# RWKV-7/gMLP block, MLA and HGRN2 on one core: the B branch's gates queued beside the inverses, and the output projection's inputs loaded one step sooner

## The chip, the cores and the metric

The kernel runs on one core of one Trainium2 chip (trn2). The metric is the device time of one execution in microseconds (us); a lower time is better. Names of engines: PE is TensorE (matmuls), DVE is VectorE, ACT is ScalarE, POOL is GpSimd, SP is SyncE, which here only issues transfers (DMA).

## The reference, cut to what matters

Two blocks run one after the other on 512 tokens of width 1024, all in float32. The change lies in the first block, whose branches share one input `h`:

```
h = x * (1 + scale) + shift                  # from silu(c) @ w_ada
p = h @ w_in                                 # 1536 columns for A, 2176 for B
out_a = gelu(u) * mix(layer_norm(gelu(v))) * silu(gate)      # A branch
# B branch, RWKV-7, 8 heads of 64, after a token shift:
S = S * w_t + (S a_t) b_t^T + v_t k_t^T ;  y_t = S r_t       # per head, over 512 tokens
y = (layer_norm(y) + bonus) * silu(gate)
o = concat(out_a, y) @ w_out
x = layer_norm(ALPHA * x + gate * o)
```

The second block (latent attention, two MLPs, HGRN2) follows with the same `x` and is not touched.

## The kernel before

Each float32 product is made of three matmuls of rounded parts (`mm3`): high weight with high activation, high with low, low with high. A weight tile of 1024x128 is loaded whole (`wload`, 512 KB, issued by SP, `raw`), rounded by ACT (`wh`, a CAST), and its remainder made by DVE (`wl`). `raw` and the pair `wh`/`wl` have three buffers each. One product of 1024x128 weights with all 512 tokens is 8 *steps* of three 128x512 matmuls; its sum lies in a PSUM tile `mm` (two buffers in this stage). `wprio` sets how far ahead of time the loads are scheduled.

The recurrence is done in 8 pieces of 64 tokens (`NC_R`). First DVE inverts 32x32 triangles for all pieces at once (`inverse`, L788: 31 pairs of multiply and add on `XT`, `TV`, `us`), and the result goes through DRAM (`scT`) to the tiles `Tst` and `TTb` of each piece (`tload`, eight loads of 16 KB; two sets of buffers, so that piece c+2 waits for piece c's `merge`). `merge(c)` makes the inverse of a 64x64 block: PE on `Tst`, DVE `Psb`, PE on `TTb`, ACT copies the result (`TTn`, named `XT` in the profile). Then PE turns `V` and `BK`, which ACT copies to `TV`, `Bt`, `Kt`. `chain(c)` is the recurrence: PE `sd`, ACT copy `ds`, PE `su`, DVE `us`, PE `ss` and `sd` again, ACT copy `Yt`, ACT and DVE update `S`.

Other products fill PE's time. They wait in a Python list `queue`; `fill(n)` takes n steps out of it into the program. While DVE inverts, `fill(NFILL)` puts in the first steps; later `chain(c)` yields three times and `fill(FILLS[c][i])` puts steps between. The queue holds four `ugate` products pairs of the A branch (4 x 16 steps) and four `gate` products of the B branch (8 steps each). `gate(i)` (L676) loads `bz` (one buffer, from DRAM `bonD`), makes its product, and at its end queues one float32 matmul of `bz` with a block matrix `bo` on PE (a *bonus matmul* below; it shows as `mg<-bz,bo`, two records), then a token shift (ACT `sh`, DVE `gsh`), a tanh and three more passes (`gt`, `gsh`, `gbn`), and writes `G2D` and `B2D` to DRAM.

`out_gate` (L931) is a part of the modulation: 512 KB of `w_ada` in `raw`, summed by DVE in eight instructions (`ga`). `operands` (L958) loads the A branch's result (`oaD`) back and splits it (ACT `aH`, DVE `aL`), after which the output projection (weights `w_out`, matmuls of 128x256) can begin on its first half; the step after which this is put in is `OPC`. All PE work of this stage carries one order token (`petoken`), so that PE keeps the order in which it is written down, except for the output projection, which the scheduler puts where it expects room. Each engine's list of instructions is fixed when the program is built.

Of the kernel before, what the change touches and what calls it, by code (L numbers as in the profile page):

```python
# [36 lines left out]
EARLY = 3  # L37
UNITS = ((0, 1), (1, 1), (2, 2), (4, 2), (6, 2))
TT = ("sm", "sm", "mm", "mm")
NFILL = 69  # L40
ORDER = "r0 A0 k1 g0 k2 r1 g0 n0 r2 f11 g0 f1 t0 g1 m0 g1 k3 g1 g2 l0 g2 r3 g3 l1 g2 f5 l2 f2 g3 l3 f3 l4 f2 g3 l5 f3 l6 f3 l7"
ORDER = [(z[0], int(z[1:])) for z in ORDER.split()]
OPC = 3
OG = (2, 2, 1, 0, 1, 0, 0, 0)
FILLS = [(0, 3, 5), (0, 3, 5), (2, 5, 3), (2, 6, 5)] + [(0, 0, 0)] * 4
HALVES = (slice(0, T // 2), slice(T // 2, T))


# [13 lines left out]
class Kern:  # L62
# [238 lines left out]
    def block1(self):  # L301
# [175 lines left out]
        def shift_evac(ps, mc, out, v3=False):  # L477

            sh = shs[0]
            shs.append(shs.pop(0))  # L480
            self.act(sh[:, 1 : T + 1], ps, AF.Copy, scale=self.pc("mu_b", mc))
            o3 = lambda a: a.rearrange("p (c t) -> p c t", t=RC) if v3 else a
            self.stt(out, o3(ps), omu[:, mc : mc + 1], o3(sh[:, 0:T]), ALU.mult, ALU.add)
# [174 lines left out]
        def part_gemm(w, col0, evac, leng=None):  # L658
            wh, wl = self.wchunk(w, col0, 8, P, leng)
            ps = self.ptl("mm")  # L660
            for k in range(8):
                self.mm3(ps, wh[:, k, :], wl[:, k, :], h.hi(k), h.lo(k), k == 0, k == 7)
                if k == 7:
                    with tc.high_priority(self.wprio):
                        evac(ps)
                yield
# [9 lines left out]
        def gate(i, pool):  # L676
            bz = self.tl(pool, [P, T], "bz", bufs=1)
            nc.sync.dma_start(out=bz, in_=bonD[i])

            def evac(ps):  # L680
                psb = self.ptl("mg")
                self.mm(psb, self.bo, bz)
                bn = self.tl(pool, [P, T], "gbn", bufs=1)
                self.tt(bn, psb, V[i], ALU.mult)
                g = self.tl(pool, [P, T], "gsh", bufs=2)
                shift_evac(ps, 12 + i, g)
                t = self.tl(pool, [P, T], "gt", bufs=2)
                self.act(t, g, AF.Tanh, scale=0.5)
                self.stt(t, t, 1.0, g, ALU.add, ALU.mult)
                self.act(t, t, AF.Copy, scale=0.5)  # L690
                self.act(g, t, AF.Copy, scale=self.pc("gn_g", i))
                nc.sync.dma_start(out=G2D[i], in_=g)
                self.stt(bn, bn, self.pc("gn_b", i), t, ALU.add, ALU.mult)
                nc.sync.dma_start(out=B2D[i], in_=bn)

            yield from part_gemm(w_in, 3072 + i * P, evac)
# [22 lines left out]
        queue = []  # L719

        def fill(n):

            while n > 0 and queue:
                if next(queue[0], "end") == "end":
                    queue.pop(0)
                else:
                    n -= 1
# [47 lines left out]
        rp = rx_.enter_context(self.pool("rw", 1))  # L775
# [190 lines left out]
        self.petoken = "block1"  # L966
        queue += [ugate(j, rp) for j in range(4)]
        self.psums([("mm", 2), ("mg", 2), ("sd", 2), ("su", 1), ("ss", 1)])
        queue.append(gate(0, rp))
        self.wprio = 3000  # L970
        fill(NFILL)
        self.wprio = 400
# [15 lines left out]
        with first():  # L988
            for _ in between(0, ()):
                pass  # L990
        for i in range(1, 4):
            queue.append(gate(i, rp))
        posts, ogs = [], []

        def start(n):
# [7 lines left out]
        for c in range(NC_R):  # L1003
            late = [posts.pop(0) for _ in range(LATE[c])]
            steps = chain(c, between(c + 1, late))
            while True:
                with first():
                    i = next(steps, None)
                if i is None:
                    break  # L1010
                fill(FILLS[c][i])
            if c in POSTS:
                posts.append(post(POSTS.index(c)))
                with first():
                    next(posts[-1])
            if c == OPC:
                while queue:
# [830 lines left out]
```

## Time and profile before

| | us |
|---|---|
| median of 3 runs | 1593.04 (1591.77 to 1593.08) |
| the profiled execution | 1593.87 |
| its span in the trace | 1591.8 |
| PE busy | 1530.3 (96%) |
| DVE busy | 908.4 (57%) |
| ACT busy | 714.2 (45%) |
| granted PE clock, mean | 0.989 |

The span is the time from the first to the last instruction of the trace; the profiled execution was about 2 us longer, and 0.8 us longer than the median. Busy time of PE is that of its matmul records, whose ends are modelled, so a busy PE is not one at its peak. Times within the trace count from the span's start. The changed stage lies between about 200 and 300 us.

### The profile page before, as it was taken

The page shows a single profiled execution, that of the slowest core. Times are in us where ns is not written, and L with a number is a line of the kernel's source. Part 1 is how long each engine was busy: PE and PEld are TensorE (multiplying, and loading weights), DVE is VectorE, ACT ScalarE, POOL GpSimd, SP SyncE. Part 2 cuts the span into 40 slices and gives each one's busy share as a digit, 9 for nine tenths or more (in the row PEclk, how much of TensorE's full clock was granted, in tenths as well). Part 3 has the DMA queues.
Part 4 walks back from the last instruction along what each step waited for, and adds up shares of the span by engine and source line. Part 5 has one row for each costly group of instructions (what it writes and reads, how often), then busy time and mean ns, then how long its engine had stood idle before and what let it go on. Part 6 is the DMA issues. An engine that isn't in the chain of part 4 may idle for free.

```text
span 1591.8 us, 21985 instructions
## 1 busy us (share of the span) xinstructions
PE 1530.3 (96%) x8389; PEld 1299.7 (82%) x8389; DVE 908.4 (57%) x1613; ACT 714.2 (45%) x1302; POOL 255.6 (16%) x418
## 2 busy tenths in 40 slices
PE   5899989989999999999999999999999999999997
PEld 4787778889878899888888887888888988888886
DVE  6767677667668738333343456667755714343445
ACT  3544226545666656332232335667645624332232
POOL 3212010324300032000000033223324100000000
PEclk9999999999999999999999999999999999999999
DMA  9632556532133133333333232322213224232421
GB/s 313 193 104 85 113 156 183 156 110 70 54 78 91 39 99 87 100 96 102 93 93 103 82 104 60 110 73 79 68 54 106 93 67 120 80 105 66 132 80 53
DMA packets 260828, 161.17 MB, mean 101 GB/s; under 512 B 29553, under 2 KB 241124, under 8 KB 260724
## 3 DMA queue, kind: packets, MB, share of 16 engines
q1 hardware_dynamic: 258036, 153.40, 33.4%
q0 software_dynamic: 2544, 6.11, 1.4%
q8 instruction: 66, 1.08, 0.3%
q14 instruction: 38, 0.31, 0.1%
q10 hardware_dynamic: 144, 0.26, 0.0%
HBM read 146.90 MB, written 11.53 MB: 100 GB/s over the span
## 4 chain that ended last, share of the span: by engine, by line
PE 68%; DVE 4%; issue 2%; ACT 1%; DMA 1%; POOL 1%; SPq 0%; DVEq 0%; POOLq 0%; ACTq 0%
PE mm L143 59%; PE sm L143 5%; PE po L143 2%; PE sc L143 1%; DVE bL L133 1%; DVE res L123 1%; DVE wl L123 1%; DMA sw<-tr 0%; PE pt L1377 0%; PE sm L149 0%; DVE mlom L133 0%; DVE hgmm L133 0%; POOL tr L123 0%; PE kv L143 0%; DVE mlpy L123 0%
## 5 line engine op out<-in xcount | busy, mean ns | idle before, releaser
L140 ACT CAST wh<-raw 128x1024 fp32r<-128x1024 f32 (+3 forms) x244 | 242.4, 995 | 475.9 <-PE mm L143 380.1
L123 DVE TENSOR_TENSOR wl<-raw,wh 128x1024 fp32r<-128x1024 f32 (+3 forms) x244 | 287.6, 1180 | 292.3 <-ACT wh L140 288.7
L143 PE MATMUL mm<-bL,wh 128*128 128x512 f32 (+1 forms) x752 | 279.1, 374 | 0.8 <-DVE bL L133 0.8
L143 PE MATMUL mm<-bH,wl 128*128 128x512 f32 (+1 forms) x752 | 278.1, 372 | 0.0
L143 PE MATMUL mm<-bH,wh 128*128 128x512 f32 (+1 forms) x752 | 276.9, 375 | 0.5 <-ACT t L137 0.4
L143 PE MATMUL mm<-aH,wh 128*128 128x512 f32 (+1 forms) x656 | 240.3, 368 | 5.8 <-ACT gsh L137 3.2
L143 PE MATMUL mm<-aL,wh 128*128 128x512 f32 (+1 forms) x656 | 238.3, 364 | 0.0
L143 PE MATMUL mm<-aH,wl 128*128 128x512 f32 (+1 forms) x656 | 237.2, 363 | 0.2 <-DVE wl L123 0.2
L143 PEld LDWEIGHTS mm<-bL,wh 128*128 128x128 f32 x752 | 141.1, 188 | 25.0 <-DVE bL L133 1.3
L143 PEld LDWEIGHTS mm<-bH,wl 128*128 128x128 f32 x752 | 141.2, 188 | 24.8
L143 PEld LDWEIGHTS mm<-bH,wh 128*128 128x128 f32 x752 | 139.4, 188 | 26.0 <-ACT t L137 0.8
L143 PEld LDWEIGHTS mm<-aH,wh 128*128 128x128 f32 x656 | 125.6, 192 | 27.5 <-ACT gsh L137 3.6
L143 PEld LDWEIGHTS mm<-aH,wl 128*128 128x128 f32 x656 | 125.6, 192 | 19.8 <-DVE wl L123 0.6
L143 PEld LDWEIGHTS mm<-aL,wh 128*128 128x128 f32 x656 | 126.0, 192 | 17.7 <-issue 0.2
L143 PE MATMUL mm<-wh,aH 128*128 128x512 f32 x288 | 113.5, 396 | 1.7 <-ACT aH L140 1.7
L143 PE MATMUL mm<-wl,aH 128*128 128x512 f32 x288 | 113.3, 395 | 0.0
L143 PE MATMUL mm<-wh,aL 128*128 128x512 f32 x288 | 109.3, 395 | 0.0
L140 ACT CAST aH<-t 128x512 fp32r<-128x512 f32 (+1 forms) x74 | 41.0, 564 | 75.2 <-DVE t L123 75.1
L143 PEld LDWEIGHTS mm<-wh,aH 128*128 128x128 f32 x288 | 54.7, 190 | 14.2 <-ACT aH L140 1.8
L123 DVE TENSOR_TENSOR aL<-t,aH 128x512 fp32r<-128x512 f32 (+1 forms) x74 | 45.0, 617 | 36.9 <-ACT aH L140 36.9
L143 PEld LDWEIGHTS mm<-wh,aL 128*128 128x128 f32 x288 | 54.4, 190 | 12.4
L143 PEld LDWEIGHTS mm<-wl,aH 128*128 128x128 f32 x288 | 54.6, 190 | 12.1
(548 smaller groups left out, 2593.5 us busy)
## 6 DMA issues: line engine op xcount, KB each, us to landing
raw<-in_mlp_w_dram SPq DMA_DIRECT2D x128, 512.0 KB
raw<-in_hgrn_w_in_dram SPq DMA_DIRECT2D x32, 512.0 KB
raw<-in_w_in_dram SPq DMA_DIRECT2D x23, 512.0 KB
ada<-in_w_ada_dram SPq DMA_DIRECT2D x16, 512.0 KB
raw<-in_w_out_dram SPq DMA_DIRECT2D x10, 512.0 KB
raw<-in_w_ada_dram SPq DMA_DIRECT2D x8, 512.0 KB
raw<-in_mla_w_o_dram SPq DMA_DIRECT2D x8, 512.0 KB
raw<-in_hgrn_w_o_dram SPq DMA_DIRECT2D x8, 512.0 KB
```

Source lines behind the costliest of these rows:

```text
L123: self.st((eng or self.nc.vector).tensor_tensor(out=out, in0=a, in1=b, op=op))
L133: self.st(self.nc.vector.scalar_tensor_tensor(out=out, in0=a, scalar=s, in1=b, op0=op0, op1=op1))
L140: self.st(self.nc.scalar.copy(out=out, in_=in_))
L143: i = self.nc.tensor.matmul(out, l, r, start=start, stop=stop, **kw)
```

## The change

All four `gate` products are put in the queue before `fill(NFILL)`, which now takes 80 steps in place of 69: the 64 of the A branch and two whole gates. The other 16 steps go between the first three pieces, 6, 6 and 4 of them (before: 8, 8, 10 and the last one). `operands` is put in after piece 2 in place of piece 3.

```
-NFILL = 69
+NFILL = 80
...
-OPC = 3
+OPC = 2
 OG = (2, 2, 1, 0, 1, 0, 0, 0)
-FILLS = [(0, 3, 5), (0, 3, 5), (2, 5, 3), (2, 6, 5)] + [(0, 0, 0)] * 4
+FILLS = [(0, 3, 3), (0, 3, 3), (0, 2, 2)] + [(0, 0, 0)] * 5
...
         queue += [ugate(j, rp) for j in range(4)]
         self.psums([("mm", 2), ("mg", 2), ("sd", 2), ("su", 1), ("ss", 1)])
-        queue.append(gate(0, rp))
+        queue += [gate(i, rp) for i in range(4)]
         self.wprio = 3000
         fill(NFILL)
...
             for _ in between(0, ()):
                 pass
-        for i in range(1, 4):
-            queue.append(gate(i, rp))
         posts, ogs = [], []
```

How this moves instructions, at three places.

**Place 1, PE and SP at the end of the fill.** On PE, before, the fifth step of gate 0 (tile `mm_1978`) is followed by the merge of piece 0:

```order
L143 MATMUL mm_1978<-aL_134,wh_1974 128x512
L143 MATMUL mm_1978<-aH_126,wl_1975 128x512
L143 MATMUL mg_2007<-Tst_1548,M_330_2002 128x64 x4
L143 MATMUL mg_2014<-TTb_1550,Psb_2012 64x128 x4
L149 MATMUL mg_2020<-ident,V_101 64x128
```

After the change the last step of gate 1 (tile `mm_2026`) and its bonus matmul stand there:

```order
L143 MATMUL mm_2026<-aH_129,wl_2023 128x512
L143 MATMUL mg_2051<-bz_2018,bo 128x512
L143 MATMUL mg_2079<-Tst_1548,M_343_2074 128x64 x4
L143 MATMUL mg_2086<-TTb_1550,Psb_2084 64x128 x4
L149 MATMUL mg_2092<-ident,V_101 64x128
```

So nine matmuls (three steps) of gate 0 and 24 of gate 1, with two bonus matmuls, moved from between the pieces to ahead of the first merge, and the merge stands behind the second load of `bz`. On SP, the loads of weights around the end of the inverse (`in_w_in` are weights of gates, `in_w_ada` is `out_gate`) change places:

```order
 L161 DMA raw_1972<-in_w_in_dram 128x8x128
-L934 DMA raw_2036<-in_w_ada_dram 128x8x128
+L161 DMA raw_2020<-in_w_in_dram 128x8x128
 L714 DMA oaD<-gt_1815 128x512
-L934 DMA raw_2047<-in_w_ada_dram 128x8x128
-L161 DMA raw_2159<-in_w_in_dram 128x8x128
+L934 DMA raw_2108<-in_w_ada_dram 128x8x128
+L934 DMA raw_2119<-in_w_ada_dram 128x8x128
 L714 DMA oaD<-gt_1889 128x512
 L806 DMA scT<-TV_1542 128x1024
```

Gate 1's weights moved ahead of two loads of `w_ada`. Some 20 loads later, behind the loads of `Tst` and `TTb` of pieces 0 and 1, SP has after the change (before, piece 2's eight loads of `Tst` and `TTb` stand between the second and the third of these rows, and no load of `bz` is there):

```order
L816 DMA Tst_1549<-scT 32x4x32
L817 DMA TTb_1551<-scT 32x4x32
L714 DMA oaD<-gt_1963 128x512
L934 DMA raw_2238<-in_w_ada_dram 128x8x128
L678 DMA bz_2018<-bonD 128x512
L934 DMA raw_2249<-in_w_ada_dram 128x8x128
L161 DMA raw_2332<-in_w_in_dram 128x8x128
L692 DMA G2D<-gsh_2007 128x512
```

The load of `bz` for gate 1 is queued behind those of pieces 0 and 1, a write of `oaD` and a load of `w_ada`.

**Place 2, DVE ahead of the first `Psb`.** `Psb` is the step of the merge that PE waits for. Before:

```order
L133 SCALAR_TENSOR_TENSOR gt_1963<-mx_1896,gt_1963 128x512
L133 SCALAR_TENSOR_TENSOR ga_339_2049<-raw_2047,sc,ga_339_2049 128x128 x3
L128 TENSOR_SCALAR ga_364_2189<-raw_2187,sc 128x128
L123 TENSOR_TENSOR Psb_2012<-mg_2007,ist 128x256
L133 SCALAR_TENSOR_TENSOR ga_364_2189<-raw_2187,sc,ga_364_2189 128x128 x7
```

After:

```order
L133 SCALAR_TENSOR_TENSOR gsh_2007<-mm_1978,omu,sh_605 128x512
L123 TENSOR_TENSOR gbn_2005<-mg_2003,V_101 128x512
L133 SCALAR_TENSOR_TENSOR gt_2010<-gt_2010,gsh_2007 128x512
L128 TENSOR_SCALAR ga_373_2240<-raw_2238,sc 128x128
L133 SCALAR_TENSOR_TENSOR gbn_2005<-gbn_2005,pb,gt_2010 128x512
L133 SCALAR_TENSOR_TENSOR ga_373_2240<-raw_2238,sc,ga_373_2240 128x128 x6
L133 SCALAR_TENSOR_TENSOR gsh_2055<-mm_2026,omu,sh_606 128x512
L133 SCALAR_TENSOR_TENSOR ga_373_2240<-raw_2238,sc,ga_373_2240 128x128
L123 TENSOR_TENSOR Psb_2084<-mg_2079,ist 128x256
```

The third load of `w_ada` (`raw_2238`, the one just ahead of `bz_2018` on SP) is now read ahead of `Psb`, with all eight instructions of its sum and parts of gates 0 and 1.

**Place 3, ACT in the recurrence, from `Yt` of piece 1 to `ds` of piece 2.** Before:

```order
L140 COPY Yt_2058<-sd_2209 64x512
L140 COPY TV_1653<-mg_2299 64x4x64 x2
L140 CAST wh_2445<-raw_2443 128x1024
L137 ACTIVATE S_1_1553<-S_0_1552,PC_105 128x128
L140 COPY Bt_1544<-mg_2306 64x4x64 x2
L140 COPY Kt_1546<-mg_2306 64x4x64 x2
L137 ACTIVATE S_1_1555<-S_0_1554,PC_106 128x128
L137 ACTIVATE S_1_1557<-S_0_1556,PC_107 128x128
L137 ACTIVATE S_1_1559<-S_0_1558,PC_108 128x128
L137 ACTIVATE gt_2274<-gt_2274 128x512
L137 ACTIVATE gsh_2271<-gt_2274,pb 128x512
L140 COPY ds_2379<-sd_2368 64x512
```

After (the last rows of the same piece; `Yt`, `TV` and the cast `aH_2522` stand ahead of them):

```order
L140 COPY Kt_1546<-mg_2366 64x4x64 x2
L137 ACTIVATE S_1_1553<-S_0_1552,PC_105 128x128
L137 ACTIVATE S_1_1555<-S_0_1554,PC_106 128x128
L140 CAST aH_2524<-raw_2538 128x512
L137 ACTIVATE S_1_1557<-S_0_1556,PC_107 128x128
L137 ACTIVATE S_1_1559<-S_0_1558,PC_108 128x128
L137 ACTIVATE gsh_2319<-gt_2322,pb 128x512
L140 CAST aH_2526<-raw_2544 128x512
L140 CAST aH_2528<-raw_2544 128x512
L140 COPY ds_2424<-sd_2413 64x512
```

A weight cast left this place, and the four casts of the A branch's result came in, all ahead of `ds`.

## Rows read from the trace of the kernel before

**Rows 1.** Windows: us; busy PE, PEld, DVE, ACT, POOL; clock; DMA share; GB/s.

```profile
213.90:235.00 21.10, 16.22 (x84) 12.87 (x84) 13.53 (x35) 6.44 (x13) 4.53 (x9) 0.84 0.60 172
235.00:300.00 65.00, 64.93 (x445) 56.19 (x444) 47.23 (x112) 39.20 (x80) 13.85 (x21) 1.00 0.71 208
```

**Rows 2.** Timeline of PE: start, us, instruction, count [idle before <-releaser].

```profile
199.65 0.39 PE L143 MATMUL mm<-aH,wh 128*128 128x512 f32 x1
...
213.70 0.39 PE L143 MATMUL mm<-aH,wl 128*128 128x512 f32 x1
217.26 0.50 PE L143 MATMUL mm<-aH,wh 128*128 128x512 f32 x1 [3.17 <-ACT gsh L137]
...
223.51 1.08 PE L143 MATMUL mg<-Tst,M 128*128 128x64 f32 x8 [0.94 <-DMA Tst<-scT]
...
236.26 1.02 PE L143 MATMUL mg<-bz,bo 128*128 128x512 f32 x2
...
243.45 1.05 PE L143 MATMUL sd<-TV,res 128*128 128x128 f32 x8
```

**Rows 3.** Windows over PE's slow stretches, columns as in rows 1.

```profile
218.80:222.10 3.30, 3.30 (x9) 2.58 (x8) 3.05 (x11) 0.00 (x0) 0.00 (x0) 0.50 0.74 186
...
225.50:229.00 3.50, 3.39 (x17) 2.48 (x16) 2.18 (x6) 1.79 (x5) 1.05 (x3) 0.52 0.23 35
```

**Rows 4.** Timeline of ACT around PE's first gap.

```profile
215.66 1.04 ACT L140 CAST wh<-raw 128x1024 fp32r<-128x1024 f32 x1 [10.62 <-DMA raw<-in_w_in_dram]
```

**Rows 5.** Timeline of SP's queue, 201 to 232 us.

```profile
201.74 0.37 SPq L934 DMA_DIRECT2D raw<-in_w_ada_dram  x1
...
211.53 0.37 SPq L161 DMA_DIRECT2D raw<-in_w_in_dram  x1
...
222.48 0.43 SPq L816 DMA_DIRECT2D Tst<-scT  x1
...
225.80 0.43 SPq L817 DMA_DIRECT2D TTb<-scT  x1
...
230.25 0.38 SPq L714 DMA_DIRECT2D oaD<-gt  x1
...
231.20 0.85 SPq L161 DMA_DIRECT2D raw<-in_w_in_dram  x1
```

**Rows 6.** Window over transfers issued at 230 to 231 us, columns as in rows 1.

```profile
232.30:236.00 3.70, 3.70 (x24) 3.11 (x23) 0.91 (x2) 0.58 (x1) 1.54 (x4) 1.00 1.04 277
```

**Rows 7.** Timeline of DVE ahead of the first merge.

```profile
218.75 1.90 DVE L133 SCALAR_TENSOR_TENSOR ga<-raw,sc,ga 128x128 f32<-128x128 f32 x5
...
224.63 0.42 DVE L123 TENSOR_TENSOR Psb<-mg,ist 128x256 f32<-128x256 f32 x1
```

**Rows 8.** Timelines of DVE, ACT and PE, piece 1 to piece 2.

```profile
248.91 0.69 DVE L123 TENSOR_TENSOR us<-su,bo 128x512 f32<-128x512 f32 x1 [0.35 <-PE su L143]
...
254.95 0.59 ACT L140 COPY Yt<-sd 64x512 f32<-64x512 f32 x1 [0.63 <-PE sd L143]
...
261.45 0.58 ACT L140 COPY ds<-sd 64x512 f32<-64x512 f32 x1
...
264.68 1.16 PE L143 MATMUL su<-ds,XT 64*128 64x128 f32 x8
...
270.41 1.65 ACT L140 CAST aH<-raw 128x512 fp32r<-128x512 f32 x3
```

**Rows 9.** Timelines of DVE, SP, ACT and PE, piece 2 to the first output products.

```profile
265.88 0.69 DVE L123 TENSOR_TENSOR us<-su,bo 128x512 f32<-128x512 f32 x1
...
272.23 1.57 SPq L161 DMA_DIRECT2D raw<-in_w_out_dram  x2
...
278.05 1.03 ACT L140 CAST wh<-raw 128x1024 fp32r<-128x1024 f32 x1
...
279.11 1.22 DVE L123 TENSOR_TENSOR wl<-raw,wh 128x1024 fp32r<-128x1024 f32 x1 [0.52 <-ACT wh L140]
...
280.91 0.28 PE L143 MATMUL mm<-aH,wh 128*128 128x256 f32 x1
```

More of the change, by code (lines that the diff above doesn't have):

```diff
@@ L39 @@
 TT = ("sm", "sm", "mm", "mm")
-NFILL = 69
+NFILL = 80
 ORDER = "r0 A0 k1 g0 k2 r1 g0 n0 r2 f11 g0 f1 t0 g1 m0 g1 k3 g1 g2 l0 g2 r3 g3 l1 g2 f5 l2 f2 g3 l3 f3 l4 f2 g3 l5 f3 l6 f3 l7"
 ORDER = [(z[0], int(z[1:])) for z in ORDER.split()]
-OPC = 3
+OPC = 2
 OG = (2, 2, 1, 0, 1, 0, 0, 0)
-FILLS = [(0, 3, 5), (0, 3, 5), (2, 5, 3), (2, 6, 5)] + [(0, 0, 0)] * 4
+FILLS = [(0, 3, 3), (0, 3, 3), (0, 2, 2)] + [(0, 0, 0)] * 5
 HALVES = (slice(0, T // 2), slice(T // 2, T))
@@ L968, in block1 @@
         self.psums([("mm", 2), ("mg", 2), ("sd", 2), ("su", 1), ("ss", 1)])
-        queue.append(gate(0, rp))
+        queue += [gate(i, rp) for i in range(4)]
         self.wprio = 3000
@@ L990, in block1 @@
                 pass
-        for i in range(1, 4):
-            queue.append(gate(i, rp))
         posts, ogs = [], []
```

## Prediction

> **What bounds the kernel now.** I read the page's busy times first: PE works in 1530.3 of 1591.8 us, so time is won only where PE is idle or slow, or lost where a change makes it idle. Then the windows around the changed stage [rows 1]: from 235 to 300 us, which is most of the recurrence, PE is busy in 64.93 of 65 us at full clock, while DVE (47 us) and ACT (39 us) have room; but from 213.9 to 235 us it is busy in only 16.2 of 21.1 us. So before the change the recurrence itself has no gap to give back; all that can be won lies in the 21 us around the end of the inverse. All that the change moves is PE work, and its amount stays: the question is where PE waits.
>
> The timeline of PE shows the gaps [rows 2]: 3.17 us until 217.26, for ACT's `gsh`, and 0.94 us until 223.51, for the loads of `Tst`. The first is no lack of work. ACT had the gelu (`gsh`) to do, but ahead of it in its list stood the cast of gate 1's weights, which waited for a transfer issued at 211.53 and landed at 215.66 [rows 4, 5]; the gelu frees the PSUM buffer that gate 0's product needs. A slow clock follows: the granted clock is 0.50 (1.2 in place of 2.4 GHz) from 218.8 to 222.1 and 0.52 from 225.5 to 229 [rows 3]; before the first fall PE had stood 3.17 us, before the second it had two shorter waits.
>
> **Prices.** A 128x512 matmul costs 0.227 us when nothing waits: 62 of them lie between the starts at 199.65 and 213.70 [rows 2]. A bonus matmul of `bz` costs 1.02 us [rows 2].
>
> **Part 1, up to the first matmul of piece 1 (`sd`, 243.45 [rows 2]).** At that point PE has done 39 gate matmuls and one bonus matmul since 213.93, where the last product of the A branch ends; after the change it has done 66 and two. The same work would be done before at 243.45 + 27 x 0.227 + 1.02 = 250.6. That is the mark to compare with. Now the changed order, step by step.
>
> *The first gap goes.* Gate 1's weights are loaded in the place of the `w_ada` load of 201.74 [rows 5], ten us earlier than at 211.53. With the 4.1 us that the load of 211.53 took until ACT used it, they are there at 206, before the buffers that the cast needs are free. So ACT does its gelu in time, gate 0 starts at 213.93 and its 24 matmuls end at 219.4, the bonus matmul at 220.4, and gate 1's 24 at 225.8. (The remainder of its weights, `wl`, keeps its place on DVE right behind the inverse, which is early enough.) This is 3.2 us won, and the clock has no reason to fall here.
>
> *A new wait takes its place.* Behind gate 1 on PE stands its bonus matmul, and behind that the whole merge. `bz` has one buffer, so its second load can only be issued after the first bonus matmul, at 220.4; but it also stands in SP's list behind 16 small loads, a write and a `w_ada` load. The small loads are issued 0.47 us apart (eight from 222.48 to 225.80 [rows 5]). Piece 2's eight, which stood ahead of the write of `oaD` at 230.25, now stand behind it, and the list may run up to 0.9 us earlier, because the entry ahead of the small loads now waits for a `wl` that comes a us sooner. So the write comes 3.9 to 4.8 us earlier, at 225.8 (middle), the `w_ada` load at 226.3 and `bz` at 226.8. What such a train takes is shown at 230.25 to 231.20 [rows 5]: write, `w_ada`, weights, of which the last two (1.05 MB) moved from 232.3 to 236.0 at 277 GB/s [rows 6], so 1.85 us for 512 KB. Shifted by 4.4 us, `w_ada` is in at 229.8 and the 256 KB of `bz` at 230.7. PE thus stands from 225.8 to 230.7, ends the bonus matmul at 231.7 and the first merge matmuls at 232.8 (1.08 us [rows 2]).
>
> *DVE is later than PE.* `Psb`, on which the merge's next matmuls wait, now stands behind a whole `out_gate` sum that reads this same `w_ada` load. From 229.8: eight instructions at 0.37 (five in 1.90 [rows 7]), 2.9 us; two 128x512 passes at 0.69 (width of `us` [rows 8]), 1.4; so `Psb` at 234.1, against 233 if PE alone set it. Ahead of ACT's copy of the merge stands, in the same way, the cast of gate 3's weights, loaded one `w_ada` and one weight load behind `bz`: 230.7 + 3.7 = 234.4, cast (1.03 [rows 9]) and a tanh of about 0.6 until 236.0, some 2 us behind `Psb`, about when PE's merge delivers; I take no cost (bound: 1 us).
>
> *From `Psb` to piece 1.* Before: 243.45 - 224.63 [rows 2, 7] = 18.8 us, with 24 gate matmuls and a bonus matmul in it (6.5 us), so 12.4 without; this includes a slow clock, and I leave it in, since PE has stood longer than before (bounds: nothing, or 1.8 us more, if nine fill matmuls fall in it at twice 0.227). After: 18 gate matmuls, 4.1 us, and one pass of a gate among ACT's copies, about 0.6 (as `Yt` [rows 8]). So piece 1 starts at 234.1 + 12.4 + 4.1 + 0.6 = 251.2, which is **0.6 us later** than the mark. Bounds: 0.45 either way for SP; if DVE does not wait, 1.2 us less.
>
> **Part 2, piece 1 to piece 2.** PE reaches `su` of piece 2 earlier after `us` of piece 1, because 12 fewer gate matmuls stand between (18 in place of 30, from the two orders): before 264.68 - 248.91 = 15.8 us [rows 8], after 15.8 - 2.7 = 13.0. `su` needs ACT's `ds`. Before, ACT got there 12.5 us after `us`, six and a half after `Yt` [rows 8], with 2.6 us to spare. Its list loses a cast of weights (1.03) and gains four `aH` at 0.55 (three in 1.65 [rows 8]): 1.2 more, so `ds` starts at 13.7 and ends at 14.3. PE waits **1.3 us**. Bounds: nothing, if ACT catches up ahead of `Yt`; 2.5, if the second load of `oaD`, issued only when DVE has freed its buffer, is late too.
>
> **Part 3, piece 2 to the output projection.** Loading the operands "one step sooner" moves little: their casts already stood at 270 us [rows 8], before the end of piece 2. What the first output products wait for is their weights. Before, the load is issued 6.35 us after `us` of piece 2 (272.23 and 265.88), is cast at 12.2, and PE comes to it at 15.0 [rows 9]. SP's list between is the same kind (a `w_ada` load, piece 5's eight, a `w_ada` load), so the load stays at 6.4 after `us`; but PE, with 15 gate matmuls fewer and one merge product (1.08) behind instead of ahead, comes to it at 15.0 - 3.4 - 1.1 = 10.5. The weights land at 6.4 + 4.1 = 10.5, are cast at 11.5 and split at 12.8 (1.22 [rows 9]), and the third matmul needs the split: PE waits about **2.0 us**. Bounds: nothing, if the load goes out 2 us sooner; 3.5, if it is late by another transfer.
>
> How long a 512 KB load takes decides here. The trace has 4.1 us (211.53 to 215.66 [rows 4, 5]), and the sum goes by that. The Trainium skill, DMA: Bandwidth & Descriptors, "Anatomy of one DMA", has a fit of 2.0 us and 436 GB/s, given for POOL's path, which no run here shows for SP's loads of weights. An estimate by that page would be 3.2 us for such a load: part 3 would be 1.1 us and the whole sum 0.9 less, 3.0 us, inside what counts as no change. The measured load was slower than the page's, so the 4.1 us stand.
>
> **The sum** is 0.6 + 1.3 + 2.0 = +3.9 us. Made on the profiled execution it gives 1597.8; that execution was 0.8 us above the median of the runs shown, so on the median 1593.04 + 3.9 = **1597 us**. Behind the stage all work hangs on the recurrence's end and shifts with it.
>
> **Rivals.**
> *The fill pays.* If `bz` were there by 225.8, and DVE's sum with it, `Psb` would stand at 225.8 + 1.0 + 1.1 = 227.9, piece 1 would start at 245.0 and 5.6 us would be won: 1587.4, or 1590.7 where parts 2 and 3 still cost 3.3. For it: a gap of 3.17 us that does go. Against: SP would have to issue `bz` about 5 us sooner, and nothing in its list allows that. It decides from a landing at about 228. Chance 0.10.
> *It comes out even.* Parts 2 and 3 are hidden, because PE's order has slack I did not see, and part 1 nets out at -0.6 to 0.6: 1592 to 1594. For it: ACT and DVE are idle a quarter to 40% of the recurrence. Against: both are late by their place in the list, not by load. Chance 0.28.
> *The clock falls again and again.* Waits of 1.3 and 2 us in the recurrence bring PE to half speed as the short waits at 222 to 225 did [rows 3]. A stretch like that from 218.8 to 222.1 holds nine matmul records [rows 3], each 0.2 us dearer at half speed: 1.8 us, so two give 1600.5. Against: where PE's waits come one by one it need not fall. Chance 0.12.
>
> **How the numbers follow.** My forecast, 1595 to 1599, has 0.50. A change within 0.2% (3.2 us) is about what a measurement cannot tell from none. Slower by more than that: two thirds of the forecast and a little more (0.35), the clock rival (0.12), and upper bounds of the even case (0.03), together 0.50; the same: the rest of the forecast (0.15), of the even case (0.25) and of the fill that pays (0.03), 0.43; faster 0.07. The range leaves out the fast rival's better half and the sum of all upper bounds: 1590.5 to 1602. The forecast's own range is 1594 to 1600.
>
> **What would show it.** Right: no gap at 214 us on PE; a gap of 4 to 6 us behind gate 1, ended by `bz`; DVE's `ga` waiting for `raw<-in_w_ada` until about 230; `su` of piece 2 waiting for ACT's `ds`; the first 128x256 matmuls waiting for `wh` or `wl` of `w_out`. Wrong: `bz` landing before 228, or PE without gaps from 251 to 300 us.

## The result, and the profile after

The changed kernel takes 1599.87 us (median of five, 1598.13 to 1605.02), the kernel before took 1592.16 us beside it (five, 1588.84 to 1593.08): ratio 1.0054, 95% interval 1.0035 to 1.0072. It is slower, by more than the 0.2% that can be told from no change.

The profiled execution of the changed kernel was the fastest of its five (1598.13 us, span 1596.0), that of the kernel before (1593.87 us) was slower than all of the five beside it. The two traces thus differ by 4.2 us, not by 7.7, and 1.2 us of the 4.2 had come about before the changed stage. So all places below are counted from one landmark, DVE's copy that ends the inverse (L807). Its row before and after, from DVE's timelines:

```profile
214.59 1.03 DVE L807 COPY XT<-TV 128x1024 f32<-128x1024 f32 x1
```

```profile
215.79 1.13 DVE L807 COPY XT<-TV 128x1024 f32<-128x1024 f32 x1
```

PE's timeline after the change shows the stage (columns as in [rows 2]; "PE stands" means that it is idle ahead of an instruction):

```profile
220.52 1.02 PE L143 MATMUL mg<-bz,bo 128*128 128x512 f32 x2
...
233.04 2.07 PE L143 MATMUL mg<-bz,bo 128*128 128x512 f32 x2 [6.01 <-DMA bz<-bonD]
234.90 1.81 PE L143 MATMUL mg<-Tst,M 128*128 128x64 f32 x8
237.23 1.09 PE L143 MATMUL mg<-TTb,Psb 128*64 128x128 f32 x8 [0.52 <-DVE Psb L123]
239.32 0.63 PE L149 MATMUL mg<-ident,V 128*64 128x128 f32 x4 [1.00 <-ACT XT L140]
...
254.08 1.05 PE L143 MATMUL sd<-TV,res 128*128 128x128 f32 x8
...
273.42 1.38 PE L143 MATMUL su<-ds,XT 64*128 64x128 f32 x8 [1.04 <-ACT ds L140]
...
286.77 0.36 PE L143 MATMUL mm<-aH,wh 128*128 128x256 f32 x1
```

The gap of 3.17 us at 214 us [rows 2] is gone. In its place PE stands 6.01 us for `bz`, then works slowly (2.07 us for a bonus matmul that took 1.02, 1.81 for the merge's 1.08), and stands 1.04 us for `ds` in piece 2, which before needed no wait [rows 8]. The first output product (286.77) waits for nothing. Between the merge and piece 1, PE stands 1.00 us for ACT's copy `XT`. ACT's timeline has the freed gelu (`gsh`, right behind a cast that waits for no load; before [rows 4]), the `aH` casts ahead of `ds`, and the cast for the first output product, done before PE comes to it:

```profile
209.62 1.05 ACT L140 CAST wh<-raw 128x1024 fp32r<-128x1024 f32 x1 [3.42 <-PE mm L143]
210.57 0.59 ACT L137 ACTIVATE gsh<-mm 128x512 f32<-128x512 f32 x1
...
271.64 1.12 ACT L140 CAST aH<-raw 128x512 fp32r<-128x512 f32 x2
272.79 0.58 ACT L140 COPY ds<-sd 64x512 f32<-64x512 f32 x1
...
284.77 1.03 ACT L140 CAST wh<-raw 128x1024 fp32r<-128x1024 f32 x1
```

The weights of the output projection are there because their load goes out early: 3.5 us after DVE's `us` of piece 2, where it went out 6.4 us after it before [rows 9]. By then DVE has done the last `aL` and so has read the A branch's result out of the `raw` buffers; the load goes out right behind piece 5's small loads. DVE's timeline and SP's queue:

```profile
273.35 0.94 DVE L123 TENSOR_TENSOR aL<-raw,aH 128x512 fp32r<-128x512 f32 x1
...
275.08 0.68 DVE L123 TENSOR_TENSOR us<-su,bo 128x512 f32<-128x512 f32 x1
```

```profile
276.73 1.73 SPq L817 DMA_DIRECT2D TTb<-scT  x4
278.56 4.07 SPq L161 DMA_DIRECT2D raw<-in_w_out_dram  x2
```

Before, DVE did the `aL` only behind `us`, the first at 270.31 and three more in the row below, and the load waited on SP for one of them (1.3 us); it went out at 272.23.

```profile
271.51 1.89 DVE L123 TENSOR_TENSOR aL<-raw,aH 128x512 fp32r<-128x512 f32 x3
```

SP's queue around the merge shows why `bz` is late: it goes out behind the small loads, the write and the `w_ada` load, at 228.65 (before [rows 5]), and lands 4.4 us later.

```profile
227.70 0.38 SPq L714 DMA_DIRECT2D oaD<-gt  x1
228.12 0.43 SPq L934 DMA_DIRECT2D raw<-in_w_ada_dram  x1
228.65 0.64 SPq L678 DMA_DIRECT2D bz<-bonD  x1
```

DVE stands for that same `w_ada` load and finishes its sum 0.4 us before PE delivers to `Psb` (before [rows 7]):

```profile
232.30 0.29 DVE L128 TENSOR_SCALAR ga<-raw,sc 128x128 f32<-128x128 f32 x1 [2.88 <-DMA raw<-in_w_ada_dram]
...
236.03 0.34 DVE L133 SCALAR_TENSOR_TENSOR ga<-raw,sc,ga 128x128 f32<-128x128 f32 x1
236.75 0.42 DVE L123 TENSOR_TENSOR Psb<-mg,ist 128x256 f32<-128x256 f32 x1 [0.38 <-PE mg L143]
```

The granted clock (windows, columns as in [rows 1]) is at its lower level (0.50, 1.2 of 2.4 GHz) when PE starts again after the stand, and once more behind the wait for `ds`; elsewhere in the recurrence it is full:

```profile
233.00:236.60 3.60, 3.56 (x10) 2.45 (x10) 3.20 (x9) 0.00 (x0) 0.00 (x0) 0.50 1.15 321
236.60:254.00 17.40, 14.72 (x99) 12.33 (x99) 5.90 (x11) 9.36 (x21) 3.41 (x8) 1.00 0.48 133
...
274.20:277.60 3.40, 3.40 (x14) 2.71 (x13) 3.23 (x10) 0.58 (x1) 0.81 (x2) 0.50 0.96 246
277.60:300.00 22.40, 22.40 (x172) 20.29 (x171) 16.31 (x40) 15.48 (x33) 6.35 (x8) 1.00 0.77 229
```

### The profile page after: what moved, and what is told of

Same layout as the page of the kernel before. It is cut to its first block, busy times and chain, and to the rows that moved or that the text cites. A ratio compares the mean times of both kernels' runs of the same rounds, so it can differ in the third digit from the quotient of the medians.

```text
span 1596.0 us, 21991 instructions
## 1 busy us (share of the span) xinstructions
PE 1529.3 (96%) x8389; PEld 1299.8 (81%) x8389; DVE 908.0 (57%) x1613; ACT 713.9 (45%) x1302; POOL 256.6 (16%) x418
## 3 DMA queue, kind: packets, MB, share of 16 engines
q8 instruction: 66, 1.08, 0.3%
## 4 chain that ended last, share of the span: by engine, by line
PE 67%; DVE 5%; issue 2%; ACT 1%; DMA 1%; POOL 1%; SPq 0%; POOLq 0%; DVEq 0%; ACTq 0%
PE mm L143 58%; PE sm L143 5%; PE po L143 2%; PE sc L143 1%; DVE bL L133 1%; DVE wl L123 1%; DVE res L123 1%; DMA sw<-tr 0%; PE pt L1375 0%; PE sm L149 0%; DVE hgmm L133 0%; DVE mlom L133 0%; POOL tr L123 0%; PE kv L143 0%; SPq L1315 0%
```

## The experiments

Three theories stood against each other. *Two losses*: the fill loses at the merge (by `bz` and by DVE's sum), the operands lose at `ds`, and the clock adds to both. *One wait*: `bz` alone is the loss. *One part*: either the fill or the operands cost everything. The table has for each kernel, from its own timelines and in us:

- `Psb`: the first `Psb`, of piece 0, counted from the landmark.
- piece 1: the first `sd` of piece 1 counted from the landmark, less the kernel before (28.86) and less the gate work done earlier (27 matmuls at 0.227 and a bonus matmul, 7.15 us, as in the prediction's mark; 3.06 us for 72 steps, 6.47 for the last row). A positive number is late for equal work.
- piece 7: `su` of the last piece, where all have done the same gates, less the kernel before (118.13). (e2 has done five more output matmuls there.)
- the measured ratio to the kernel before, run beside it.

| kernel | `Psb` | piece 1 | piece 7 | ratio (95% interval) |
|---|---|---|---|---|
| before | 10.04 | 0 | 0 | 1 |
| changed | 20.96 | +2.3 | +4.8 | 1.0054 (1.0035 to 1.0072) |
| e1, `bz` early | 20.71 | +3.4 | +4.6 | 1.0032 (1.0020 to 1.0043) |
| e2, fill alone | 21.67 | +4.0 | +6.1 | 1.0037 (1.0024 to 1.0049) |
| e3, operands alone | 9.95 | -0.4 | +6.9 | 1.0037 (1.0021 to 1.0054) |
| e4, 72 steps | 13.47 | +7.7 | +10.2 | 1.0063 (1.0047 to 1.0079) |
| e5, `Psb` first | 20.42 | +1.5 | +5.5 | 1.0051 (1.0034 to 1.0067) |
| e6, one early sum | 10.34 | +0.7 | +2.2 | 1.0014 (1.0003 to 1.0024) |
| e7, 72 steps, `Psb` first | 8.48 | -3.3 | +9.1 | 1.0058 (1.0044 to 1.0073) |
| e8, own `gbn` | 15.81 | -3.1 | 0.0 | 1.0019 (1.0006 to 1.0032) |
| e9, 72 steps, casts later | 9.33 | +6.8 | +13.1 | 1.0112 (1.0097 to 1.0128) |
| e10, e8 and casts later | 13.33 | -1.9 | -0.7 | 1.0022 (1.0010 to 1.0034) |
| e11, e10, 5+5+6 steps | 13.38 | +0.6 | +1.7 | 1.0018 (1.0007 to 1.0030) |

Each kernel has one trace. The changed kernel and e2 hold the same instructions in the same order up to piece 1, and yet e2 is 1.7 us later there; its clock is at 0.50 from 230.8 to 244.5 us, that of the changed kernel from 229.8 to 236.7. So differences of less than about 2 us between rows of the table show nothing.

**e1.** The changed kernel; `bz` of gates 1 and 2 in the two buffers of tag `mx`.

```
-            bz = self.tl(pool, [P, T], "bz", bufs=1)
+            bz = self.tl(pool, [P, T], "mx", bufs=2) if i in (1, 2) else self.tl(pool, [P, T], "bz", bufs=1)
```

> The changed kernel, with the bz tiles of gates 1 and 2 in buffers of another tag, so that the load of bz need not wait for the first bonus matmul. Theory (PE's wait for bz hides a second wait, of DVE's Psb for the third sum of w_ada): the stand of 6.0 us ahead of the second bonus matmul shrinks below 1 us, but PE then stands some 5 us ahead of TTb's matmuls, because Psb stays at 235 to 236.5; piece 1 starts at most 1.2 us earlier, and the time is 1598.5 to 1600 where the changed kernel has 1599.9. Rival (bz alone is the loss): Psb at about 231, piece 1 some 5 us earlier, the time 1594 to 1596.

`Psb` did not move (20.71 against 20.96). PE and DVE now, from their timelines:

```profile
231.12 0.28 DVE L128 TENSOR_SCALAR ga<-raw,sc 128x128 f32<-128x128 f32 x1 [1.98 <-DMA raw<-in_w_ada_dram]
...
234.19 0.42 DVE L123 TENSOR_TENSOR Psb<-mg,ist 128x256 f32<-128x256 f32 x1
```

```profile
234.66 1.97 PE L143 MATMUL mg<-TTb,Psb 128*64 128x128 f32 x8 [6.60 <-DVE Psb L123]
```

The stand of 6.01 us for `bz` became one of 6.60 us for `Psb`, which waits behind the sum of a `w_ada` load. *One wait* is refuted. The ratio is lower than the changed kernel's, but the intervals overlap, and at piece 7 the traces agree within 0.2 us.

Two more readings of e1 are used below: the wait for `ds` in piece 2, and the load of the output projection's weights against PE's coming to the first output product. DVE's, SP's and PE's rows:

```profile
273.85 0.68 DVE L123 TENSOR_TENSOR us<-su,bo 128x512 f32<-128x512 f32 x1
```

```profile
276.50 3.52 SPq L161 DMA_DIRECT2D raw<-in_w_out_dram  x2
```

```profile
272.19 1.16 PE L143 MATMUL su<-ds,XT 64*128 64x128 f32 x8 [1.04 <-ACT ds L140]
...
284.15 0.36 PE L143 MATMUL mm<-aH,wh 128*128 128x256 f32 x1
```

PE comes to the first output product 10.3 us after `us`, the load goes out 2.65 us after `us`, and that product waits for nothing.

**e2 and e3.** The two parts apart: the changed kernel with `OPC = 3`, and the kernel before with `OPC = 2`.

> The changed kernel with its fill, but the operands put in after piece 3 as before. Theory (two losses of about equal size, one in the fill, one from the operands' casts ahead of ds): su of piece 2 waits less than 0.3 us for ds, no slow clock between 265 and 280 us, and the time is 1595 to 1597.5, 2.5 to 4 us below the changed kernel. Rival A (the fill alone is the loss): 1599 to 1600.5. Rival B (the operands alone are the loss): 1591.5 to 1593.

> The kernel before with its fill, but the operands put in after piece 2. Theory (the casts are late only because the change took 12 gate matmuls from ahead of su; before there were 2.6 us to spare): ds is ready within 0.5 us of PE, and the time is 1591 to 1594, the same as before. Rival (the operands cost by themselves): a wait of 1 to 2 us ahead of su of piece 2 with a slow clock behind it, 1595 to 1597.

e2 is as its theory said in the trace: `su` of piece 2 does not wait, because two of the four `aH` casts stand ahead of `ds` in place of all four, and PE is at full clock (1.00 from 272 to 278 us). ACT's and PE's rows of e2:

```profile
272.31 1.12 ACT L140 CAST aH<-raw 128x512 fp32r<-128x512 f32 x2
273.45 0.58 ACT L140 COPY ds<-sd 64x512 f32<-64x512 f32 x1
```

```profile
274.08 1.16 PE L143 MATMUL su<-ds,XT 64*128 64x128 f32 x8
```

Its ratio is 0.17% below that of the changed kernel, but the intervals overlap. So of *one part*, that the operands are everything is refuted, since the fill alone costs 0.37%; that the fill is everything is not refuted by the times. What the operands add is shown by the traces only: the wait for `ds`, in the changed kernel and e1 and not in e2.

e3 should have cost nothing and costs 0.37% too. Its `su` of piece 2 waits for nothing, but this does not test the theory: the scheduler put all four `aH` casts behind `ds` there, as in the kernel before [rows 8]. What waits are the first output products, for `wh` and `wl` of `w_out`, and a long slow stretch follows. ACT's and PE's timelines and a window of e3:

```profile
261.95 0.58 ACT L140 COPY ds<-sd 64x512 f32<-64x512 f32 x1
...
269.93 0.62 ACT L140 CAST aH<-raw 128x512 fp32r<-128x512 f32 x1 [0.87 <-DMA raw<-in_w_ada_dram]
...
281.79 1.04 ACT L140 CAST wh<-raw 128x1024 fp32r<-128x1024 f32 x1 [1.90 <-DMA raw<-in_w_out_dram]
```

```profile
282.88 0.39 PE L143 MATMUL mm<-aH,wh 128*128 128x256 f32 x1 [1.62 <-ACT wh L140]
...
284.40 0.39 PE L143 MATMUL mm<-aH,wl 128*128 128x256 f32 x1 [0.75 <-DVE wl L123]
```

```profile
285.00:295.20 10.20, 10.20 (x46) 9.30 (x45) 6.71 (x15) 3.48 (x5) 6.68 (x8) 0.50 0.74 207
```

Waits of 1.62 and 0.75 us, then 10.2 us at clock 0.50. The wait is the one of the prediction's part 3, but not for its reason. PE comes to the product 14.8 us after `us` of piece 2 (266.45), as before (15.0 [rows 9]) and not early; the load goes out 9.6 us after `us` (276.02, before 6.4), because the `w_ada` load ahead of it on SP waited 4.8 us for a sum of DVE.

**e4.** The changed kernel with 72 steps, gate 1 between the pieces.

```
-NFILL = 80
+NFILL = 72
...
-FILLS = [(0, 3, 3), (0, 3, 3), (0, 2, 2)] + [(0, 0, 0)] * 5
+FILLS = [(0, 3, 5), (0, 3, 5), (0, 4, 4)] + [(0, 0, 0)] * 5
```

> The changed kernel with 72 steps in the fill in place of 80 (gate 0 whole, gate 1 between the pieces), and the first three pieces with 8, 8 and 8 steps. Theory (PE stands for the second bz and the third sum of w_ada; without a second bonus matmul ahead of the merge it waits for neither): no stand of over 2 us between 220 and 235 us, piece 1 starts at most 0.5 us behind the kernel before measured by equal work, and with the casts still ahead of ds the time is 1592 to 1596. Rival (the first gap of 3.17 us returns, or DVE's sum still stands ahead of Psb): 1596 to 1600.

Not better than the change (1.0063, the intervals overlap), and 10.2 us late at piece 7: the theory's 1592 to 1596 is far off. No second bonus matmul stands ahead of the merge, but the gap for `gsh` is back (3.04 us), and ACT's cast of a later gate's weights, waiting for its load, stands ahead of `Bt` and `Kt`:

```profile
233.77 1.04 ACT L140 CAST wh<-raw 128x1024 fp32r<-128x1024 f32 x1 [1.21 <-DMA raw<-in_w_in_dram]
```

```profile
217.43 0.80 PE L143 MATMUL mm<-aH,wh 128*128 128x512 f32 x1 [3.04 <-ACT gsh L137]
...
236.27 1.42 PE L143 MATMUL ss<-TV,Kt 128*128 128x128 f32 x8 [3.18 <-ACT Kt L140]
```

**e5, e8, e10, e11.** The fill with `OPC = 3`, one wait after the other taken away. e5: e1's edit, and the first `Psb` ahead of all sums by an order token on DVE. e8: for gate 1 `gbn` in a buffer of its own as well (and `bz` only for gate 1). e10: casts of later weights behind ACT's copy of the first merge. e11: e10 with other steps.

```
+            self.token = "inverse" if c == 0 else None        # e5, around Psb
             self.tt(Psb, q4(ps[:, : 4 * RC]), ist.unsqueeze(1).to_broadcast([P, 4, RC]), ALU.add)
+            self.token = None
...
-                bn = self.tl(pool, [P, T], "gbn", bufs=1)     # e8
+                bn = self.tl(pool, [P, T], "mx", bufs=2) if i == 1 else self.tl(pool, [P, T], "gbn", bufs=1)
...
+            self.token = "xt" if c == 0 else None             # e10, and on later casts of weights
             self.copy(at(TTn[c % 2]), ps2[0:64, :])
+            self.token = None
...
-FILLS = [(0, 3, 3), (0, 3, 3), (0, 2, 2)] + [(0, 0, 0)] * 5
+FILLS = [(0, 2, 3), (0, 2, 3), (0, 3, 3)] + [(0, 0, 0)] * 5
```

> The changed fill with the operands after piece 3 (as in the run of the fill alone), bz of gates 1 and 2 in buffers of another tag, and the first Psb kept ahead of all sums of w_ada on DVE by an order token. Theory (the fill loses only by two waits, for bz and for DVE's sum of w_ada, and pays once both are gone): no stand of over 1.5 us on PE between 214 and 235 us, Psb at 229 to 231, full clock from 235 to 265 us, and 0 to 4 us below the kernel before of the same call, some 6 us below the fill alone. Rival A (the work comes too early for the recurrence in any case, so that its copies and loads are late): 2 us or more above the kernel before. Rival B (the sums that were pushed behind Psb make us or wl late in the recurrence): a new stand of over 1 us on PE between 235 and 300 us that DVE ends, 2 to 5 us above the kernel before.

> The run with the first Psb kept ahead of all sums, and now gate 1's gbn in a buffer of its own too (that of another tag), because there DVE stood 4.5 us for the write of gate 0's gbn, with Psb behind it. Theory (three waits stood one behind the other: bz, the sum of w_ada, and the one buffer of gbn; with the third gone the fill pays up to the recurrence): Psb at 230.5 to 232.5 us, PE's stand ahead of TTb below 3 us, piece 1's first sd at 247 to 250 us where that run has 254, and 3 to 7 us below that run (0.5% above the kernel before), so within 0.2% of the kernel before or up to 0.2% below it. Rival A (a fourth wait takes the place): Psb after 234 us, behind another load or buffer. Rival B (the early gain is given back in the pieces, because the sums and gate 3's weights come later): Psb early, but piece 4's su no more than 2 us earlier than in that run, and the time over 0.3% above the kernel before.

> The run with the gbn buffer, and on ACT the casts of later weights kept behind the copy of the first merge by an order token, because there the evacuation of gate 0 stood behind the cast of gate 2's weights (landed at 224 us), and Psb behind that on DVE. Theory (a fourth wait): Psb at 228.5 to 230.5 us, PE's stand of 3.2 us ahead of TTb below 1.5 us, piece 1 some 2 us earlier, and 1 to 3 us below the run with the gbn buffer, level with the kernel before or up to 0.15% below it. Rival (gate 2's weights or the sums are then late in pieces 0 and 1, and the pieces give back what the merge wins): a new stand of over 1 us between 232 and 265 us, and no lower than the run with the gbn buffer.

> The same with the 16 steps of gates 2 and 3 put between the pieces as 5, 5 and 6 in place of 6, 6 and 4, so that piece 2 has more of PE's work beside its waits. Theory: the small stands of piece 2 (0.85 us for Psb, 0.4 for issue) shrink, and 0 to 1.5 us below the other run of this call. Rival: the pieces are set by ACT and DVE, and the time is within 1 us of the other run.

In e5 no sum stands ahead of `Psb`, and `Psb` is still at 20.42. DVE stands for the write of gate 0's `gbn`, whose only buffer gate 1 needs (`B2D`, in SP's list behind the small loads):

```profile
236.29 0.69 DVE L123 TENSOR_TENSOR gbn<-mg,V 128x512 f32<-128x512 f32 x1 [4.54 <-DMA B2D<-gbn]
236.90 0.41 DVE L123 TENSOR_TENSOR Psb<-mg,ist 128x256 f32<-128x256 f32 x1
```

```profile
237.37 1.97 PE L143 MATMUL mg<-TTb,Psb 128*64 128x128 f32 x8 [7.87 <-DVE Psb L123]
```

A third wait, so e5's theory of two fell. With the third gone (e8) PE's stand falls from 7.87 to 3.21 us and `Psb` comes 4.6 us sooner; piece 1 is 3.1 us ahead of equal work, and the ratio falls to 1.0019. Up to piece 1 the fill does pay. At piece 7 that is lost again. From `sd` of piece 1 to `su` of piece 7 PE is idle for 4.9 us in e8, partly in small waits that the kernel before does not have (0.85 us for `Psb`, 0.51 and 0.42 of its own issue), and for 2.8 us in the kernel before; that is 2.0 of the 3.1 us. The stand ahead of `TTb` is still 3.21 us, in e8:

```profile
232.08 1.97 PE L143 MATMUL mg<-TTb,Psb 128*64 128x128 f32 x8 [3.21 <-DVE Psb L123]
```

e10 takes that away too, and PE then waits 0.80, 2.33 and 1.64 us, for `Psb`, for the copy of the merge and for `TV`, because gate 1's passes, and behind the copy a cast of weights, stand ahead of these on ACT. One of the passes stands 3.21 us for a write of `gt`, a fifth wait in the row:

```profile
234.62 0.63 ACT L137 ACTIVATE gt<-gsh 128x512 f32<-128x512 f32 x1 [3.21 <-DMA oaD<-gt]
```

```profile
237.16 0.66 PE L149 MATMUL mg<-ident,BK 128*128 128x128 f32 x4 [2.33 <-ACT XT L140]
239.45 0.97 PE L143 MATMUL sd<-TV,res 128*128 128x128 f32 x4 [1.64 <-ACT TV L140]
```

The time did not fall further (1.0022, 1.0018). In e10 the rival held: new stands of over 1 us. e11 is 0.9 us below e10, which fits its theory and its rival alike. (e10's profiled execution, 1598.77 us, is long although its trace is 0.7 us ahead at piece 7, because its landmark lies at 219.38, 4.8 us later than before.)

**e6, e7, e9.** The kernel before with one early sum of `w_ada` in place of two, which brings gate 1's weights one place forward; e7 also with 72 steps and e5's token, e9 with 72 steps and e10's token.

```
-OG = (2, 2, 1, 0, 1, 0, 0, 0)
+OG = (2, 2, 2, 0, 1, 0, 0, 0)
...
-        start(2)
+        start(1)
```

> The kernel before with one sum of w_ada started ahead of the recurrence in place of two (the other after piece 2), so that gate 1's weights are loaded one place earlier. Theory (the stand at 214 us lies beside the way of the inverse through DRAM, which sets the first merge): the stand for gsh at 214 us falls from 3.2 us below 0.5, PE stands some 4 us ahead of Tst's matmuls in its place, and the time is within 1.5 us of the kernel before. Rival (the stand at 214 us is lost time, as the prediction's part 1 took it): Tst's matmuls start 2 to 3 us earlier and the time falls by 2 to 4 us.

> The kernel before with one early sum of w_ada in place of two, 72 steps in the fill (gate 0 whole with its bonus matmul, 3.1 us more work ahead of the merge), and the first Psb ahead of all sums of w_ada by an order token. Theory (the time between the inverse and Tst's landing is 4 us of idle PE, and 3.1 us of work that waits for nothing fits in): no stand of over 1.5 us between 214 and 235 us, piece 1's start level with the kernel before although 3.1 us more is done, and 2 to 4 us below the kernel before. Rival (ACT's casts and DVE's sums, now later, are late for the pieces): a stand of over 1 us between 228 and 260 us, and the time from 1 us below to 5 us above the kernel before.

> The kernel before with one early sum of w_ada in place of two, 72 steps in the fill, and on ACT the casts of later weights kept behind the copy of the first merge by an order token (Psb without a token). Theory (5.45 us of PE's idle time ahead of Tst's matmuls take 3.1 us of work, if no cast or sum stands ahead of the merge's own steps): piece 1 starts within 0.5 us of the kernel before although 3.1 us more is done, and if gate 1's weights are not late for piece 0, 1 to 3 us below the kernel before. Rival (gate 1's weights, now cast behind the merge, make PE stand in piece 0): a stand of over 1 us for wh or wl between 228 and 236 us, a slow clock behind it, and 0 to 5 us above the kernel before.

e6 shows what the first gap was worth by itself: nothing. It is gone, and PE stands for `Tst` in its place:

```profile
224.40 1.94 PE L143 MATMUL mg<-Tst,M 128*128 128x64 f32 x8 [5.45 <-DMA Tst<-scT]
```

`Psb` comes at 10.34 from the landmark, before at 10.04: the way of the inverse through DRAM sets it. (At 1.0014 e6 is within the 0.2% of the kernel before.) e7 fills these 5.45 us with 3.1 us of work, and up to piece 1 it gains as its theory said (-3.3). Its copies and loads are late all the same, as its rival said: PE stands for the merge's copy at 239 us (1.12), for `ds` in piece 1 (1.16), for `TV` at 281 us (1.09) and for `wh` at 292 us (0.72). Two stretches are slow, 250 to 257 us and 287.5 to 298 us (both 0.51). The wait for `ds`:

```profile
250.05 2.07 PE L143 MATMUL su<-ds,XT 64*128 64x128 f32 x8 [1.16 <-ACT ds L140]
```

e9 is the slowest (1.0112), 18 us above the kernel before, more than its rival's 5: ACT's cast of gate 2's weights waits 3.92 us for its load ahead of `Bt` and `Kt`, and PE stands 5.15 us for `Kt`. (Its rival had named gate 1's weights, and a wait for `wh` or `wl`.) No version here beats the kernel before.

## Why the prediction came out as it did

*The sum and the sign.* Forecast +3.9 us; the trace, from the landmark to piece 7, has +4.8, and the medians +7.7. Slower was right. The median of 1599.87 us lies inside the forecast's own range of 1594 to 1600, at its very end, and outside the 1595 to 1599 that it also gives. What follows goes by the trace.

*Part 1, right in mechanism, too small: 2.3 us in place of 0.6 (4.0 in e2, which is the same up to there).* The first gap went, `bz` took its place, DVE stood for the `w_ada` load beside it. Counted from the landmark (1.2 us later than before), `bz` was issued at 227.45 where the prediction had 226.8, and landed after 4.4 us where it had 3.9: together 1.1 us. The Trainium skill, DMA: Bandwidth & Descriptors, "Anatomy of one DMA", has 2.0 us and 436 GB/s, given for POOL's path. An estimate by that page is 2.6 us for 256 KB; the 4.4 us measured here, beside a `w_ada` load, speak against using it for SP. The rest is the clock: from the start of the bonus matmul to the end of the first merge matmuls there are 3.7 us where the prediction counted 2.1. It had a slow clock only in the figure taken over for the way from `Psb` on. So PE, not DVE, set `Psb`, 1.4 us later than the forecast's 234.1. From `Psb` to `sd` the term came out, 17.3 us for 17.1, but by luck: the slow clock that it took over from before did not come (1.00 from 236.6 us), and in its place PE stood 1.00 us for `XT`, 0.30 for `gbn` and 0.85 for `Kt`, none of which it does in the kernel before. The first is the cost that the prediction put at nothing, with a bound of 1 us.

*Behind it stood more than I had seen.* The prediction named two that are late together, `bz` and the sum. e1, e5 and e8 show three in a row, and the third, the single buffer of `gbn`, it did not have. A fourth and a fifth came out behind these, in e8 and e10. The rival "the fill pays" lacked it too: its condition, `bz` and the sum in time, was met in e5, and `Psb` came only 0.5 us sooner.

*Part 2, right: 1.04 us, forecast 1.3.* `su` waits for `ds` behind the `aH` casts. e2 confirms the cause: the fill is the same, two of the casts are gone from there, and so is the wait. (e3 cannot: its casts stand behind `ds`.) Not in the sum was the slow stretch that follows (274.2 to 277.6 us at 0.50, 14 matmul records), which adds up to 1.7 us, half of its 3.4. That was the rival "the clock falls again and again", which priced such a stretch at 1.8 us: here it happened beside the forecast, not in place of it. It does not belong to the wait for certain: e1 has the same wait of 1.04 us and no slow stretch behind it.

*Part 3, the step that failed: 0 in place of 2.0 us.* The step is "the load stays at 6.4 after `us`". It went out 3.5 us after `us`, because loading the operands sooner, which "moves little" in the prediction, let their `raw` buffers come free before `us` in place of behind it. That is the prediction's own bound, "nothing, if the load goes out 2 us sooner". PE also came later than forecast, 11.7 us after `us` in place of 10.5, behind the slow stretch of part 2; by the prediction's sum this alone would have left about 0.8 us of the wait (an estimate: 2.0 less 1.2). e1 shows that the load decides: PE comes at 10.3 there, as forecast, the load goes out at 2.65, and there is no wait. With this fill and the operands after piece 3 (e2, e5, e8, e10) the load goes out 5.9 to 6.3 us after `us`, so it is the operands' place that moves it (e11, with other steps between the pieces, has 4.3). The wait that e3 has there is no sign for part 3: PE is not early in e3, and the load is later than before.

So the sum of 3.9 was near by luck: the 2.0 that did not come in part 3 were made up by 1.7 more in part 1 and 1.7 behind part 2, a slow stretch that e1 does not have.

*What stays open.* The medians differ by about 3 us more than the stage does in the traces. In the five executions of the changed kernel the span grows as the mean clock falls (1596.0 us at 0.988, 1602.9 at 0.983), but only one was profiled, so where the slow stretches of the others lie is not shown. Of the 4.8 us at piece 7 some 1.8 are given back by 366 us (the same instructions are 6.0 us later than before at 340 us and 4.2 us at 366 us). Most of it is the clock: the kernel before has a slow stretch from 362.1 to 365.6 us (0.51), and the changed kernel does the same work at full clock; why the clock fell in one and not in the other is not shown. How much the operands cost in time beside the fill is open too.

## What to carry to other kernels

Before work is put into a gap, find what ends the gap once the named wait is gone: here the gap for `gsh` lay beside the inverse's way through DRAM, and removing the wait alone gained nothing. Moving a step ahead moves its single buffers, its loads and its evacuation ahead too, and on engines that work in order each of these can stand in front of the critical step; list them all (`bz`, the sum, `gbn`, the cast, the write of `gt`: five here), since taking away one shows only the next. Price a wait on PE with the slow clock that may follow. For a load, ask when its buffer comes free in the new order, and not only what stands ahead of it in the list: here the operands, put in one step sooner, also gave their buffers back sooner.

## What the runs showed of the hardware

A short wait can cost several times itself: in e3 two waits of 2.4 us in all were followed by 10.2 us at granted clock 0.50, in the changed kernel one of 1.04 us by 3.4 us at 0.50, while the kernel before worked from 235 to 300 us at 1.00 [rows 1]. It need not: behind the same wait of 1.04 us, e1 works on at full clock. Its window:

```profile
272.10:284.00 11.90, 11.71 (x81) 10.05 (x81) 8.63 (x22) 6.41 (x16) 1.68 (x3) 1.00 0.80 218
```

Executions of one program differ by more than this change: the kernel before ran from 1588.68 to 1597.39 us in the 22 runs beside e1 to e4, and the landmark itself lies between 213.5 and 219.4 us in the traces of the thirteen kernels.
